# Low parts of every fourth feed-forward weight chunk by an adding DMA, and four chunks held as parts, in a two-layer encoder trunk

## The chip, the cores and the metric

The kernel runs on one core of one Trainium2 chip. The metric is the device time of one execution in microseconds (us); the time of before is the median of three runs.

## The reference

Input x is [1, 256, 2048] in float32: 256 positions, 2048 features. Layer 0 is a mixer (a Conformer convolution beside a gated spatial unit, one input and one output projection) and a SwiGLU feed-forward; layer 1 is a Fourier mixer with a linear map, and a second feed-forward; a final RMSNorm follows. Of it, what the change touches is the feed-forward, with D_FF = 5632:

```python
def swiglu(h, w_gate, w_up, w_down):
    return (jax.nn.silu(h @ w_gate) * (h @ w_up)) @ w_down

h = rms_norm(x, ffn_norm_g[layer])
x = x + swiglu(h, ffn_w_gate[layer], ffn_w_up[layer], ffn_w_down[layer])
```

All of it is to float32 accuracy.

## The kernel before, in words

Activations lie with features on the partitions and the 256 positions on the free axis, so each 128x128 weight tile is the stationary operand of TensorE as it lies in memory. A float32 product is carried by three passes: each operand is split exactly into a high and a low part of at most 12 significant bits (float32r), and TensorE accumulates wh*xh, wh*xl and wl*xh. In `product` (L252) the first two are one pass of 512 columns with wh stationary (L257), the third is one pass of 256 columns with wl stationary (L258). `products` and `extend` (L261 to L273) do the same with three passes of 256 columns. So of each weight tile TensorE needs wh first and wl right behind it.

The weights are one stream of 656 chunks (`NCHUNK`) in the order of use. A chunk is eight weight tiles side by side, 128 partitions x 1024 float32, 512 KB. `Weights.load` (L97) does three things for a chunk: SyncE issues the transfer into a `raw` tile (L104), ScalarE casts it to the high part `whi` (L105), and VectorE subtracts the high part from the raw chunk, which gives the low part `wlo` (L106). `Weights.chunk` (L133) loads chunks until three beyond the one in use are in hand (AHEAD = 3), and hands out the chunk in use. There are four `raw` buffers (RAWS) and three buffers each of `whi` and `wlo` (PARTS). With three, the parts of chunk c are written into the buffers of chunk c-3, so the cast of c waits until TensorE has done with c-3, that is, until it starts on chunk c-2. The framework puts the instructions of each engine into a fixed order when the program is built, by their dependences and buffers; on the chip each engine takes its instructions strictly in that order and waits at semaphores.

The stream is used in this order: the mixer of layer 0 (96 chunks), the first feed-forward (264 chunks), the map of the Fourier mixer (32 chunks), the second feed-forward (264 chunks). In `ffn` (L329) each of the 44 tiles j of the hidden layer takes 2 chunks for the gate and 2 for the up product (176 chunks in all), then `joined` (L286, called twice), a sigmoid (L340), two products on VectorE (L341, L342) and a split of the result into an operand `h` (L278, L280). The 16 tiles m of the down product take the other 88 chunks, each followed by `residual` (L318) and the next norm's operand (`part_of_norm`, L165 and L167, and the squares, L189 and L196).

Operands come from one pool of 2 KB tiles per partition, tag `op`, with 60 buffers (KF + KD, L82). A feed-forward fills all of them: 16 of the norm's operand and 44 of `h`. Between the two feed-forwards the Fourier mixer reads two constant matrices; `dsp` (L625) holds the parts of one of them, 8 KB per partition in the constant pool, written from a `raw` buffer by L633 and L634 and read by `positions` (L667 to L669). GpSimd does little in this kernel: constants at the start, and the power -0.5 of the norms' means (L301, 14 times).

Of the kernel before, what the change touches and what calls it, by code (L numbers as in the profile page):

```python
"""Two-layer hybrid encoder trunk (conv + spatial gating, then FNet), float32, one core.

Activations live on chip with features on the partitions and the 256 positions on the free
axis, so that every weight matrix is the stationary operand as it lies in memory and no
activation has to be transposed.  A float32 product is carried by three single passes of
TensorE: each operand is split exactly into two parts of at most 12 significant bits (float32r),
x = xh + xl and w = wh + wl, and wh*[xh | xl] (one 512 column pass) and wl*xh are accumulated in
float32.  The norms' factors per position commute with the products and are applied to their
results, so that TensorE doesn't wait for them.
"""  # L10
# [7 lines left out]
F32 = mybir.dt.float32  # L18
# [6 lines left out]
S = 256            # positions  # L25
NB = S // P        # blocks of 128 positions
D = 2048
KD = D // P        # 16 feature tiles
DFF = 5632
KF = DFF // P      # 44  # L30
CD = 1024
KC = CD // P       # 8
TAPS = 31
PAD = 15
GD = 256           # channels of an FNet group
NG = D // GD
NV = CD // 512
CH = 8             # weight tiles of 128x128 to a chunk
AHEAD = 3          # chunks that are split ahead of the one in use
RAWS, PARTS = 4, 3 # chunks in flight as they come, and as their two parts  # L40
NMISC = 3          # PSUM banks beside those of the products with the weights
PAIRS = 11         # pairs of the convolution's taps whose products are ScalarE's
OPEN = 5           # output tiles of the first projection that stay in PSUM between its parts
LAST = 2           # convolution tiles that are taken in last for them
# the pace of the work beside the products in the first mixer, in chunks (ticks)
BUDGET = 2.0       # VectorE's work beside the split of a chunk
LATE = 1           # pairs of tiles by which the squares of x come after its split
R_AT = 4           # the first norm's factors
DELAY = 3          # before TensorE reads what VectorE is to have done
GAP = 2            # between the steps of a chain over several engines  # L50
NORM_GAP = 3       # the same in the convolution's norm
NCHUNK = (4 * KD * KC + 2 * KC * KD + KD * KD + 2 * 3 * KD * KF) // CH
RMS_EPS = 1e-6
LN_EPS = 1e-5

# columns of the packed vectors that lie along the partitions
# [10 lines left out]
def trunk(ctx, tc, xT, vec, sgu_gb, sgu_bs, sgu_wT, w, dft_c, dft_s, out):  # L67
# [12 lines left out]
    def op(dt=F32R, shape=(P, 2 * S), name="op"):  # L80
        """A 2 KB tile: an operand's two parts, or what lives beside them."""
        return acts.tile(list(shape), dt, name=name, tag="op", bufs=KF + KD)  # L82

# [6 lines left out]
    # ---- weights: one stream of chunks in the order of use, split ahead of it, and the work that  # L90
    # goes on beside the products, in the order in which the engines take it up ----
    class Weights:
        def __init__(self):
            self.loaded, self.used, self.ready = 0, 0, []
            self.tick, self.tasks, self.later, self.credit = 0, [], [], 0.0

        def load(self, pieces=1):  # L97
            raw = raws.tile([P, CH * P], F32, name="raw")
            hi = wts.tile([P, CH * P], F32R, name="whi")
            lo = wts.tile([P, CH * P], F32R, name="wlo")  # L100
            n = CH * P // pieces
            for i in range(pieces):
                c = slice(i * n, (i + 1) * n)
                nc.sync.dma_start(raw[:, c], w[self.loaded][:, c])  # L104
                nc.scalar.copy(hi[:, c], raw[:, c])  # L105
                nc.vector.tensor_sub(lo[:, c], raw[:, c], hi[:, c].bitcast(F32))  # L106
            self.loaded += 1
            self.ready.append((hi, lo))

        def start(self, task, ticks=1):  # L110
            """A generator to be taken up in so many ticks; it yields the ticks until its next part
            and what the part before is to VectorE."""
            self.tasks.append((self.tick + ticks, task))

        def step(self):
            """One tick: the parts that are due, and then of the work without haste what fits."""
            self.credit = min(self.credit, 0.0) + BUDGET
            due = [x for x in self.tasks if x[0] <= self.tick]
            self.tasks = [x for x in self.tasks if x[0] > self.tick]
            for _, task in due:  # L120
                r = next(task, None)
                if r is not None:
                    self.credit -= r[1]
                    self.start(task, r[0])
            while self.later and self.credit > 0:
                cost = next(self.later[0], None)
                if cost is None:
                    self.later.pop(0)
                else:
                    self.credit -= cost  # L130
            self.tick += 1
# [38 lines left out]
    class Norm:  # L170
        """An RMSNorm over the features: its operand's parts, without the factor per position, as
        the residual's tiles come in.  The squares are summed up by VectorE in all tiles but the
        last."""
# [5 lines left out]
        def parts(self, k, x):  # L179
            """In two parts, the second for VectorE."""  # L180
# [71 lines left out]
    def product(xs):  # L252
        """sum over tiles of w.T @ x: columns 0:S and S:2S of a PSUM bank are its two parts."""
        acc = ps.tile([P, 2 * S], F32, name="acc")
        for k, x in enumerate(xs):
            wh, wl = next(stream)
            nc.tensor.matmul(acc, wh, x, start=k == 0, stop=False)  # L257
            nc.tensor.matmul(acc[:, :S], wl, x[:, :S], start=False, stop=k == len(xs) - 1)  # L258
        return acc

    def products(xs, n):  # L261
        """n sums over tiles, side by side, each in one part."""
        accs = [ps.tile([P, 2 * S], F32, name="acc")[:, :S] for _ in range(n)]
        extend(accs, xs)
        return accs
# [9 lines left out]
    def split(dst, x):  # L275
        """x in its two float32r parts."""
# [9 lines left out]
    def joined(acc, name, scale):  # L286
        """The two parts of a product added, and scaled per position."""
# [8 lines left out]
    def inv_std(means, eps):  # L296
        """(mean + eps) ** -0.5 of [128 positions, 2] means."""
# [6 lines left out]
    def add_cols(m, x, one, first, last):  # L304
        """Add to m [128 positions, 2] the sums over the partitions of x [128, 256]."""
# [4 lines left out]
    def along_free(r):  # L310
        """[128, 2] per position to [128, 256], the same in each partition."""
# [6 lines left out]
    def residual(m, acc, bias=None):  # L318
        """The product's two parts (and a bias) onto the residual's tile m."""
# [42 lines left out]
    def convolution(j, y):  # L362
        """The depthwise convolution of y.  Of 2 * PAIRS taps ScalarE forms the products."""
# [34 lines left out]
    def group_norm(j):  # L398
        """LayerNorm over the group's channels, without its gain and bias."""
# [45 lines left out]
    # spatial gating: v with the positions on the partitions  # L445
# [43 lines left out]
    # W_s (n g + b) + b_s = (W_s n) g + b rowsum(W_s) + b_s, whose gain and bias lie on partitions  # L489
# [90 lines left out]
    # the output projection: first what comes from the gating, then from the convolution  # L580
# [40 lines left out]
    # cos of channels 0..128 and sin of 1..127 hold all of a real group's channel transform  # L621
# [3 lines left out]
    dsp = const.tile([P, 2, NB, 2, S], F32R, name="dsp")  # L625
# [6 lines left out]
    for f in range(2):  # L632
        nc.scalar.copy(dsp[:, f, :, 0, :], dsr[:, f])  # L633
        nc.vector.tensor_sub(dsp[:, f, :, 1, :], dsr[:, f], dsp[:, f, :, 0, :].bitcast(F32))  # L634
# [26 lines left out]
    def positions(g, ab):  # L661
        pq = bank()
        for f in range(2):
            o = pq[:, f * S:(f + 1) * S]
            for b in range(NB):
                ah, al = ab[0][:, b, f * P:(f + 1) * P], ab[1][:, b, f * P:(f + 1) * P]
                nc.tensor.matmul(o, ah, dsp[:, f, b, 0, :], start=b == 0, stop=False)  # L667
                nc.tensor.matmul(o, ah, dsp[:, f, b, 1, :], start=False, stop=False)
                nc.tensor.matmul(o, al, dsp[:, f, b, 0, :], start=False, stop=b == NB - 1)  # L669
# [58 lines left out]
def _tiles(k, *mats):  # L728
    """Matrices [K, M] as tiles [128, 128] in the order of use: for each output tile, for each
    matrix, over K."""  # L730
# [4 lines left out]
def _side_by_side(w, n):  # L735
    """The tiles of groups of n output tiles, over K and within the group."""
# [69 lines left out]
```

## Time and profile before

| what | value |
|---|---|
| runs | 1925.70, 1927.16, 1912.75 us; median 1925.7 |
| profiled execution: span from its first to its last instruction | 1913.1 us |
| what lies around that span, against the median | 12.6 us |
| TensorE (PE) busy | 1890.0 us, 99% of the span |
| VectorE (DVE) busy | 1270.8 us, 66% |
| ScalarE (ACT) busy | 984.1 us, 51% |
| GpSimd (POOL) busy | 17.4 us, 1% |
| SyncE's DMA queue | 347.73 MB, 55.2% of 16 engines' span |

The profiled execution has no total time of its own listed; its span is given, and the difference to the median of the runs is taken for what lies around. PE is the engine's matmuls, PEld its weight loads, which overlap the matmuls. A matmul's end in the profile is modelled and rows of consecutive matmuls overlap, so TensorE's pace is read from the starts or from counts, not from the mean duration.

### The profile page before, as it was taken

The numbers are of one execution on the slowest core, as the hardware profiler recorded it, in microseconds if no ns is written. First come the engines' busy times: TensorE is split into PE (matmuls) and PEld (weight loads), VectorE is DVE, ScalarE is ACT, GpSimd is POOL, SyncE is SP. The second block draws the span as 40 slices with busy tenths as digits, with TensorE's granted clock in tenths as the row PEclk, the third lists the DMA queues.
The fourth block names the chain that finished last, engine by engine and source line by source line (L and its number), as shares of the span: only waits on it lengthen the run. The fifth ranks groups of instructions, "written<-read, shape, count | busy, mean of one in ns | idle before, by whom it ended". The sixth has DMA issues, their size and how long they took to land.

```text
span 1913.1 us, 29269 instructions
## 1 busy us (share of the span) xinstructions
PE 1890.0 (99%) x11520; PEld 1680.2 (88%) x11520; DVE 1270.8 (66%) x1860; ACT 984.1 (51%) x1504; POOL 17.4 (1%) x46
## 2 busy tenths in 40 slices
PE   8999999999999999999999999999999999999997
PEld 8989999888888888888888888888888888888887
DVE  7999856666666666655555776666666666655554
ACT  8988745444444444444444654444444444444442
POOL 0000000000000000000000000000000000000000
PEclk9999999999999999999999999999999999999999
DMA  7555554555555555555556255555555555555553
GB/s 246 168 165 164 165 180 168 193 188 189 191 193 187 189 191 192 188 188 190 194 188 196 86 187 177 188 191 193 187 189 191 191 189 188 191 193 188 188 190 129
DMA packets 98321, 351.56 MB, mean 184 GB/s; under 512 B 11268, under 2 KB 12420, under 8 KB 98184
## 3 DMA queue, kind: packets, MB, share of 16 engines
q1 hardware_dynamic: 97464, 347.73, 55.2%
q8 instruction: 90, 1.47, 0.3%
q10 hardware_dynamic: 720, 1.97, 0.3%
q14 instruction: 47, 0.39, 0.1%
HBM read 347.54 MB, written 2.10 MB: 183 GB/s over the span
## 4 chain that ended last, share of the span: by engine, by line
PE 97%; DVE 1%; ACT 1%; issue 0%; DMA 0%; POOL 0%; SPq 0%; POOLq 0%; DVEq 0%; ACTq 0%
PE acc L257 54%; PE acc L258 27%; PE acc L271 4%; PE acc L273 4%; PE acc L272 4%; PE acc L484 1%; PE acc L485 1%; PE acc L486 1%; PE m L307 0%; DMA raw<-in_w 0%; DVE wlo L106 0%; PE m L314 0%; ACT whi L105 0%; PE m L667 0%; DVE res L723 0%
## 5 line engine op out<-in xcount | busy, mean ns | idle before, releaser
L257 PE MATMUL acc<-op,whi 128*128 128x512 f32 x4436 | 1541.9, 394 | 1.0 <-ACT whi L105 1.0
L258 PE MATMUL acc<-op,wlo 128*128 128x256 f32 x4436 | 1230.5, 278 | 0.1
L106 DVE TENSOR_TENSOR wlo<-raw,whi 128x1024 fp32r<-128x1024 f32 (+1 forms) x659 | 803.9, 1220 | 565.4 <-ACT whi L105 562.7
L105 ACT CAST whi<-raw 128x1024 fp32r<-128x1024 f32 (+1 forms) x659 | 688.2, 1044 | 876.4 <-issue 506.6
L257 PEld LDWEIGHTS acc<-op,whi 128*128 128x128 f32 x4436 | 832.4, 188 | 195.4 <-ACT whi L105 1.3
L258 PEld LDWEIGHTS acc<-op,wlo 128*128 128x128 f32 x4436 | 833.7, 188 | 1.1 <-DVE wlo L106 0.7
L271 PE MATMUL acc<-op,whi 128*128 128x256 f32 x684 | 196.8, 288 | 6.2 <-ACT whi L105 5.7
L273 PE MATMUL acc<-op,wlo 128*128 128x256 f32 x684 | 194.2, 285 | 1.3 <-DVE wlo L106 1.2
L272 PE MATMUL acc<-op,whi 128*128 128x256 f32 x684 | 194.9, 285 | 0.0
L271 PEld LDWEIGHTS acc<-op,whi 128*128 128x128 f32 x684 | 132.3, 194 | 7.2 <-ACT whi L105 6.0
L273 PEld LDWEIGHTS acc<-op,wlo 128*128 128x128 f32 x684 | 131.9, 193 | 1.9 <-DVE wlo L106 1.9
L272 PEld LDWEIGHTS acc<-op,whi 128*128 128x128 f32 x684 | 132.5, 194 | 0.5 <-DVE op L167 0.2
L375 ACT ACTIVATE op<-op,vt 128x256 f32<-128x256 f32 x168 | 72.4, 499 | 0.0
L289 ACT COPY l<-acc 128x256 f32<-128x256 f32 x176 | 64.8, 368 | 0.0
L392 DVE TENSOR_TENSOR op<-op 128x512 f32<-128x512 f32 x80 | 53.8, 684 | 1.6 <-ACT op L375 1.2
L278 ACT CAST op<-a 128x256 fp32r<-128x256 f32 x112 | 43.9, 398 | 10.3 <-DVE a L543 9.4
L280 DVE TENSOR_TENSOR op<-a,op 128x256 fp32r<-128x256 f32 x112 | 46.3, 419 | 2.0 <-ACT op L278 1.8
L292 DVE TENSOR_TENSOR a<-a,nR 128x256 f32<-128x256 f32 x88 | 37.5, 426 | 6.5 <-ACT nR L210 3.5
L292 DVE TENSOR_TENSOR b<-b,nR 128x256 f32<-128x256 f32 x88 | 37.5, 426 | 3.0
L342 DVE TENSOR_TENSOR a<-a,b 128x256 f32<-128x256 f32 x88 | 37.4, 425 | 3.0
L341 DVE TENSOR_TENSOR a<-a,s 128x256 f32<-128x256 f32 x88 | 36.9, 419 | 0.0
L291 DVE TENSOR_TENSOR b<-acc,l 128x256 f32<-128x256 f32 x88 | 36.7, 417 | 0.0
(121 smaller groups left out, 708.7 us busy)
## 6 DMA issues: line engine op xcount, KB each, us to landing
raw<-in_w SPq DMA_DIRECT2D x655, 512.0 KB, 3.4
res<-in_xT SPq DMA_DIRECT2D x7, 256.0 KB, 6.6
out<-res ACTq DMA_DIRECT2D x3, 512.0 KB, 2.8
raw<-in_w SPq DMA_DIRECT2D x4, 128.0 KB, 3.2
op<-in_sgu_wT SPq DMA_DIRECT2D x2, 256.0 KB, 3.4
raw<-in_dft_s SPq DMA_DIRECT2D x1, 512.0 KB
res<-in_xT SPq DMA_DIRECT2D x2, 128.0 KB, 2.5
raw<-in_dft_c SPq DMA_DIRECT2D x1, 256.0 KB
```

The lines of the kernel that those rows point to most:

```text
L105: nc.scalar.copy(hi[:, c], raw[:, c])
L106: nc.vector.tensor_sub(lo[:, c], raw[:, c], hi[:, c].bitcast(F32))
L257: nc.tensor.matmul(acc, wh, x, start=k == 0, stop=False)
L258: nc.tensor.matmul(acc[:, :S], wl, x[:, :S], start=False, stop=k == len(xs) - 1)
L271: nc.tensor.matmul(acc, wh, x[:, :S], start=first and k == 0, stop=False)
L272: nc.tensor.matmul(acc, wh, x[:, S:], start=False, stop=False)
L273: nc.tensor.matmul(acc, wl, x[:, :S], start=False, stop=last and k == len(xs) - 1)
L280: nc.vector.tensor_sub(dst[:, n:2 * n], x, dst[:, :n].bitcast(F32))
L289: nc.scalar.copy(t, acc[:, S:])
L292: nc.vector.tensor_mul(y, y, scale)
L375: nc.scalar.activation(t[:, f * S:(f + 1) * S], src, AF.Copy, scale=wc)
L392: nc.vector.tensor_add(sums, sums, t)
```

## The change

Two more helpers in `Weights` and two constants decide which chunks are treated otherwise: of the two feed-forwards each chunk whose number is divisible by 4 (EVERY), without the first and the last 8 chunks of each (CH = 8 is taken as the margin). For such a chunk VectorE's subtraction is gone. ScalarE writes the negated high part into `wlo` behind its cast, and GpSimd issues a transfer of the same 512 KB that adds the chunk onto `wlo`: from the weights in HBM in the first feed-forward, from the `raw` tile in SBUF in the second. PARTS goes from 3 to 4 for all chunks. The 8 KB for it come from `dsp`, which becomes four tiles of the pool `op`. The sums and their results are the same. Comments are left out below.

```diff
-RAWS, PARTS = 4, 3
+RAWS, PARTS = 4, 4
+EVERY = 4
...
+NFFN = 3 * KD * KF // CH
+FFN = (NCHUNK - 2 * NFFN - KD * KD // CH, NCHUNK - NFFN)
...
+        def summed(self, i):
+            return i % EVERY == 0 and any(a + CH <= i < a + NFFN - CH for a in FFN)
...
                 nc.sync.dma_start(raw[:, c], w[self.loaded][:, c])
                 nc.scalar.copy(hi[:, c], raw[:, c])
-                nc.vector.tensor_sub(lo[:, c], raw[:, c], hi[:, c].bitcast(F32))
+                if self.summed(self.loaded):
+                    nc.scalar.activation(lo[:, c], hi[:, c].bitcast(F32), AF.Copy, scale=-1.0)
+                    src = w[self.loaded][:, c] if self.loaded < FFN[1] else raw[:, c]
+                    nc.gpsimd.dma_start(lo[:, c], src, accum_op=ALU.add)
+                else:
+                    nc.vector.tensor_sub(lo[:, c], raw[:, c], hi[:, c].bitcast(F32))
...
-    dsp = const.tile([P, 2, NB, 2, S], F32R, name="dsp")
+    dsp = [[op(shape=(P, 2, S)) for _ in range(NB)] for _ in range(2)]
...
     for f in range(2):
-        nc.scalar.copy(dsp[:, f, :, 0, :], dsr[:, f])
-        nc.vector.tensor_sub(dsp[:, f, :, 1, :], dsr[:, f], dsp[:, f, :, 0, :].bitcast(F32))
+        for b in range(NB):
+            d = dsp[f][b]
+            nc.scalar.copy(d[:, 0], dsr[:, f, b])
+            nc.vector.tensor_sub(d[:, 1], dsr[:, f, b], d[:, 0].bitcast(F32))
```

The three matmuls of `positions` read `dsp[f][b][:, 0]` and `dsp[f][b][:, 1]` in the same places.

## Rows read from the trace of the kernel before

**Rows 1.** The page: engines' busy time, slices, and the chain that ended last.
```profile
PE 1890.0 (99%) x11520; PEld 1680.2 (88%) x11520; DVE 1270.8 (66%) x1860; ACT 984.1 (51%) x1504; POOL 17.4 (1%) x46
...
PE 97%; DVE 1%; ACT 1%; issue 0%; DMA 0%; POOL 0%; SPq 0%; POOLq 0%; DVEq 0%; ACTq 0%
```
**Rows 2.** Windows: stretch, span, busy of PE, PEld, DVE, ACT, POOL (count), clock, DMA, GB/s.
```profile
500.00:700.00 200.00, 200.00 (x1156) 174.83 (x1155) 135.38 (x199) 96.87 (x145) 0.00 (x0) 1.00 0.58 190
700.00:900.00 200.00, 200.00 (x1156) 174.82 (x1155) 122.55 (x163) 91.76 (x124) 0.00 (x0) 1.00 0.57 190
...
1600.00:1800.00 200.00, 200.00 (x1156) 174.90 (x1155) 113.09 (x139) 89.64 (x112) 0.00 (x0) 1.00 0.59 190
```
**Rows 3.** Waits of TensorE: us in total, times, longest.
```profile
PE acc L271 <- ACT whi L105: 5.7, 2, 5.5
...
PE acc L273 <- DVE wlo L106: 1.2, 2, 0.9
PE acc L257 <- ACT whi L105: 1.0, 1, 1.0
```
**Rows 4.** Timeline of TensorE in the first down product: start, us, line.
```profile
857.20 0.27 PE L258 MATMUL acc<-op,wlo 128*128 128x256 f32 x1
857.31 0.40 PE L257 MATMUL acc<-op,whi 128*128 128x512 f32 x1
```
**Rows 5.** Timeline of ScalarE and VectorE there: start, us, line [idle before].
```profile
857.39 1.05 ACT L105 CAST whi<-raw 128x1024 fp32r<-128x1024 f32 x1 [1.68 <-PE acc L257]
860.17 1.05 ACT L105 CAST whi<-raw 128x1024 fp32r<-128x1024 f32 x1 [1.73 <-PE acc L257]
...
858.47 1.23 DVE L106 TENSOR_TENSOR wlo<-raw,whi 128x1024 fp32r<-128x1024 f32 x1 [1.50 <-ACT whi L105]
```
**Rows 6.** Timeline of ScalarE in the first gate and up products.
```profile
599.52 1.05 ACT L105 CAST whi<-raw 128x1024 fp32r<-128x1024 f32 x1 [1.45 <-issue]
600.48 0.41 ACT L340 ACTIVATE s<-a 128x256 f32<-128x256 f32 x1
602.29 1.05 ACT L105 CAST whi<-raw 128x1024 fp32r<-128x1024 f32 x1 [1.41 <-issue]
```
**Rows 7.** Groups by line and shape, of VectorE and ScalarE: busy us, mean ns | idle before.
```profile
L106 DVE TENSOR_TENSOR wlo<-raw,whi 128x1024 fp32r<-128x1024 f32 x655 | 802.3, 1225 | 564.8 <-ACT whi L105 562.2
...
L278 ACT CAST op<-a 128x256 fp32r<-128x256 f32 x112 | 43.9, 398 | 10.3 <-DVE a L543 9.4 <-DVE a L676 0.9
...
L165 ACT ACTIVATE op<-res,vt 128x256 fp32r<-128x256 f32 x64 | 31.5, 505 | 3.2 <-DMA res<-in_xT 2.0 <-DVE res L326 0.8 <-DVE res L583 0.3
```
**Rows 8.** The loads of weights (L104): all their landings, from issue.
```profile
DMA to landing us min/median/max: 2.9/3.4/7.0
```
**Rows 9.** GpSimd's power (L301): duration in ns, min/median/max.
```profile
L301 POOL TENSOR_TENSOR is_r<-is_v,mhalf x14: 690/1068/1641, 27.1 to 1902.5; 128x2 f32<-128x2 f32 x14
```
**Rows 10.** The Fourier mixer's start: writing of dsp (duration ns, starts), and its first reader.
```profile
L633 ACT CAST dsp<-raw x2: 607/611/615, 1046.9 to 1048.2; 128x512 fp32r<-128x512 f32 x2
...
1048.94 1.29 DVE L634 TENSOR_TENSOR dsp<-raw,dsp 128x512 fp32r<-128x512 f32 x2
1052.70 0.16 DVE L299 TENSOR_SCALAR is_v<-m 128x2 f32<-128x2 f32 x1 [2.48 <-PE m L307]
```

More of the change, by code (lines that the diff above doesn't have):

```diff
@@ L666, in positions @@
                 ah, al = ab[0][:, b, f * P:(f + 1) * P], ab[1][:, b, f * P:(f + 1) * P]
-                nc.tensor.matmul(o, ah, dsp[:, f, b, 0, :], start=b == 0, stop=False)
-                nc.tensor.matmul(o, ah, dsp[:, f, b, 1, :], start=False, stop=False)
-                nc.tensor.matmul(o, al, dsp[:, f, b, 0, :], start=False, stop=b == NB - 1)
+                nc.tensor.matmul(o, ah, dsp[f][b][:, 0], start=b == 0, stop=False)
+                nc.tensor.matmul(o, ah, dsp[f][b][:, 1], start=False, stop=False)
+                nc.tensor.matmul(o, al, dsp[f][b][:, 0], start=False, stop=b == NB - 1)
         return pq
```

## The prediction

> **What bounds the kernel now.** I read the page first: TensorE is busy for 1890.0 of 1913.1 us, and the chain that ended last is TensorE's for 97% [rows 1]. The reader is to see that no other engine has a share to give. Then the windows inside the two feed-forwards, to ask whether TensorE's pace depends on anything around it: in 200 us it starts 1156 matmuls while VectorE is busy for 135.38, for 122.55 or for 113.09 us, always with PE busy for all 200 us and the clock at 1.00 [rows 2], the upper level, 2.4 GHz. That is 0.346 us to a tile (two matmuls) and 2.77 us to a chunk, four chunks 11.09 us. VectorE's load can fall by 22 us in a window and TensorE doesn't go faster. Last the waits of TensorE: all that it ever waited for casts or low parts is 5.7 + 1.2 + 1.0 = 7.9 us [rows 3], and the lines L271 and L273 there belong to the mixers and the last tile. So in the feed-forwards weights come early enough, and work taken from VectorE is worth nothing by itself.
>
> **How early.** In the down product TensorE starts a chunk at 857.31 [rows 4], and 0.08 us later the cast begins that had waited for the buffer of the chunk just done; the next cast is one chunk, 2.78 us, behind it [rows 5]. With three buffers that cast is for the chunk that is used two chunks on, at 857.31 + 5.55 = 862.86. Its low part is ready at 858.47 + 1.23 = 859.70 [rows 5]: 3.2 us to spare.
>
> **The change part by part.**
>
> *Subtractions removed.* Summed chunks are 62 in each feed-forward (42 in gate and up, 20 in down): 124 x 1.225 = 152 us off VectorE [rows 7]. By the windows above this is worth 0.
>
> *Negations added.* 124 on ScalarE, each 128x1024. The cast of that size takes 1.05 us [rows 5]; a 128x256 activation with a scale takes 0.505 where the cast takes 0.398 [rows 7], so 1.05 to 1.16; I take 1.15, 143 us in all. ScalarE is busy for 96.87 of 200 us in a gate and up window [rows 2], 5.4 of 11.09 us, and goes to 6.5 of 11.09: hidden, as long as its order lets the casts come in time. What is queued behind a negation is at most the next cast, which waits 2.77 us for its buffer anyway, and one small instruction of 0.41 us [rows 6].
>
> *Four buffers of parts.* The cast of chunk c now goes when TensorE starts on chunk c-3, and c is used three chunks later, 8.32 us. For an ordinary chunk the spare time grows from 3.2 to 5.9 us. For a summed one: cast 0.08 to 1.13, negation to 2.28, and 8.32 - 2.28 = 6.0 us are left for the adding transfer, from the moment GpSimd may issue it until TensorE must have the low part (5.6 if one small instruction stands between). This margin is the number that the forecast hangs on. In the mixers four buffers can only loosen casts; the most there is to win is the 7.9 us of [rows 3], and the likeliest is near nothing, since the longest of them, 5.5 us, is a cast early in the kernel.
>
> *The adding transfer.* The trace shows none, so I bound it. From below: a plain load of 512 KB lands 3.4 us after its issue [rows 8]. From above: GpSimd takes 1.07 us for even a tiny instruction, 1.64 at most [rows 9]; the transfer must read twice as much as a plain load (the source and `wlo`); and it shares the 16 engines with the raw loads. These are at 0.58 in the windows [rows 2], and with four loads in 11.09 us one load is 0.58 x 11.09 / 4 = 1.6 us of all engines. So the upper bound is 1.64 + 3.4 + 1.6 for the second read + 1.6 for one raw load that is interleaved = 8.2 us. Nearest to it is the plain load behind a start on GpSimd: 1.07 + 3.4 = 4.5 us if the second read overlaps the first, 6.1 if it comes on top. I take the middle, 5.3 us, an estimate. It is under the margin by 0.7 us (0.3 behind a small instruction), so TensorE finds the low part there: cost 0. At the ends: 3.4 gives 0 too, since an earlier landing buys nothing; 8.2 gives 124 x 2.2 = 273 us.
>
> The trace has TensorE's wait on low parts at 1.2 us in all and no adding transfer to time [rows 3]. The Trainium skill, page "Collectives: The Full Stack", section "The bandwidth ceiling: the fold count and why AG ≠ RS ≠ AR", states that a reducing transfer is limited by its two source reads, which go through one ring, and so runs at half the rate of a copy. No run here shows it yet. By it the second read doesn't overlap, the transfer takes the 6.1 us of the upper of my two values or more, and the sum would stand at the edge of the margin: 0.1 us over the 6.0, or 0.5 over the 5.6 behind a small instruction, 12 to 62 us. That is a word against the change, and the first rival below is its consequence.
>
> *Room on the transfer engines.* Each summed chunk adds 1.6 to 3.2 us of all 16 engines in 11.09 us: 0.58 becomes 0.72 to 0.87. Under 1, and a raw load has time: its buffer comes free with the subtraction of four chunks before. In the second feed-forward `raw` is held until the sum has landed, some 7.6 us after its cast instead of 2.4; three other buffers go on turning, and SyncE waits longer at its head without ScalarE finding a chunk missing. I cost it at 0; uncovered it is the second rival.
>
> *dsp in the operands' pool.* It is written between 1046.9 and 1050.2, the norm's factors after it only reach VectorE at 1052.70 [rows 10], and its reader is later still. Its four tiles now wait for `h` tiles that the last down product reads first. The same 2 x 0.61 and 2 x 0.65 us of work, in halves; 0, at worst 2 us once.
>
> *Sum.* 0 + 0 + 0 (or up to -7.9) + 0 + 0: span 1913.1 us, and with the 12.6 us around it the median, 1925.7. A measurement here tells about 1% (19 us) from no change; the three runs shown lie 0.75% apart.
>
> **The rivals.**
>
> *A: the sum lands late (slower).* Place: the first low part of each summed chunk, 124 times. Nothing recovers such a wait, since the cast of the next summed chunk is itself released by TensorE. If the second read comes on top and half a raw load is interleaved, the transfer takes 1.07 + 3.4 + 1.6 + 0.8 = 6.9 us, 0.9 over the margin: 124 x 0.9 = 112 us, 2037. It decides from 6.15 us on (0.155 x 124 = 19 us). For it: DMA is already at 0.58, landings reach 7.0 us [rows 8]. Against: that maximum is one of 659, the median is 3.4.
>
> *B: held raw buffers delay the second feed-forward.* If the load four chunks on takes the very buffer that is held, a loop closes: load 3.4, cast 1.05, negation 1.15, sum 5.3, starts 0.3 = 11.2 us against 11.09, which is nothing; with a sum of 6.0 us it is 0.8 x 62 = 50 us, 1976. Against: four buffers, of which three are free in time.
>
> *C: the transfer engines become the bound.* The room is 0.42 x 11.09 = 4.7 us per summed chunk. If adding costs as much as four plain loads, 6.4 us, it is 1.7 x 124 = 211 us over, 2137. Nothing in the trace speaks for so much.
>
> *D: a small gain.* Four buffers end all 7.9 us of waits: 1918, which is within 1%.
>
> **How the numbers follow.** Forecast 0.50, with a range of its own from 1912 to 1945 (the waits of the mixers on one side, a sum that is 0.15 us late on the other). A 0.29, B 0.08, C 0.06, D 0.07, of which 0.04 for a measurement that shows it as over 1%. Faster 0.04; same 0.50 + 0.03 = 0.53; slower 0.29 + 0.08 + 0.06 = 0.43. The range goes from 1908 to 2070: above it lie C and the upper third of A, below it next to nothing, under 0.2 together.
>
> **What would show it right or wrong.** Right: windows in the feed-forwards still with 1156 matmuls in 200 us, no TensorE wait at L258, VectorE about 152 us less, ScalarE about 143 us more, DMA between 0.72 and 0.87 there. The landing of GpSimd's transfers, by the listing of DMA issues, should be under 6 us. Wrong: a wait of L258 on a DMA, 124 or 62 times (A or B), fewer matmuls in a window, casts that wait for raw loads, or a DMA share near 1 (C).

## The result and the profile after

The changed kernel takes 1973.6 us, median of four runs (1968.5 to 1974.2). Against the kernel before, of which there are now four runs with a median of 1919.9 us, it is slower by a ratio of 1.0275, 95% interval 1.0234 to 1.0317. The profiled execution took 1968.5 us for a span of 1966.7 us: only 1.8 us lie around a span, not the 12.6 us that the table ahead of the prediction takes. What those 12.6 us were comes below.

The page after, to be laid beside [rows 1]; the third and fourth lines are the transfer queues (packets, MB, share of 16 engines), the last two the landings (median us from issue).
```profile
PE 1915.3 (97%) x11520; PEld 1689.9 (86%) x11520; DVE 1126.8 (57%) x1738; ACT 1105.1 (56%) x1630; POOL 125.3 (6%) x170
...
PE 75%; DMA 10%; issue 9%; ACT 3%; DVE 2%; POOL 0%; SPq 0%; POOLq 0%; DVEq 0%; ACTq 0%
...
q1 hardware_dynamic: 97464, 347.73, 50.6%
q0 software_dynamic: 17856, 65.02, 19.1%
...
wlo<-in_w POOLq DMA_DIRECT2D x62, 512.0 KB, 5.9
wlo<-raw POOLq DMA_DIRECT2D x62, 512.0 KB, 4.8
```
The reader is to see three things. DMA and "issue" now stand in the chain that ended last, with 19% together; before, TensorE had 97% of it. TensorE lies idle for 1966.7 - 1915.3 = 51.4 us, before for 23.1 us: 28.3 us of the 53.6 us by which the span grew are idle time. And it is busy for 25.3 us longer with the same 11520 matmuls: most of that is pace, and the rest, as the late chunk below shows, is a part of the waits that the rows count as busy.

TensorE's waits after (L269 and L270 are now the lines of the high and the low passes, L257 and L258 before), for [rows 3], and windows after, for [rows 2] (stretch, span, busy of PE, PEld, DVE, ACT, POOL, clock, DMA, GB/s).
```profile
PE acc L270 <- DMA wlo<-in_w: 25.7, 26, 1.5
...
PE acc L270 <- DMA wlo<-raw: 1.7, 1, 1.7
```
```profile
600.00:800.00 200.00, 194.88 (x1103) 168.49 (x1102) 110.47 (x173) 108.31 (x156) 14.86 (x17) 1.00 0.79 226
...
1400.00:1600.00 200.00, 200.00 (x1133) 173.33 (x1133) 112.63 (x178) 112.35 (x160) 15.50 (x18) 1.00 0.78 231
```
The waits are in the first feed-forward, where the sum reads HBM; the second, where it reads the raw tile, has one in all. But the second isn't free either. There TensorE is busy for 200 of 200 us at a granted clock of 1.00 and starts 1133 matmuls, where before it started 1156 [rows 2]: a tile takes 0.353 us and not 0.346. That costs some 14 us in a feed-forward of 2112 tiles, and no wait shows it.

One late chunk of the first feed-forward, in the chain that ended last (start, us, what); ahead of it the low pass that waited, with its neighbours, from TensorE's timeline.
```profile
521.09 0.39 PE L269 MATMUL acc<-op,whi 128*128 128x512 f32 x1
522.27 0.39 PE L270 MATMUL acc<-op,wlo 128*128 128x256 f32 x1 [0.80 <-DMA wlo<-in_w]
522.50 0.39 PE L269 MATMUL acc<-op,whi 128*128 128x512 f32 x1
```
```profile
512.89 0.83 ACT whi L111
513.72 0.13 issue
513.85 0.15 ACT op L290
514.00 0.15 issue
514.16 1.06 ACT wlo L114
515.22 0.29 issue
515.51 6.72 DMA wlo<-in_w
522.23 0.04 issue
522.27 0.22 PE acc L270
```
The cast, one small instruction of ScalarE (L290), the negation until 515.22, 0.29 us until GpSimd starts, and a transfer of 6.72 us. The low pass follows its high pass by 0.23 us elsewhere, so it was wanted at 521.32 and is 0.95 us late. From the end of the negation to that point there were 6.1 us.

The row of that wait says 0.80 us, but from 521.09 to 522.50 two passes take 1.41 us that take 0.35 elsewhere: the wait cost 1.06. The end of the pass ahead is modelled, and the difference counts as busy time. By the starts of L269 in the whole trace the two feed-forwards lost some 34 us at waits and some 21 us by pace (7 in the first, 13 in the second), and the rest of the kernel gave 1 us back.

### The profile page after: what moved, and what is told of

Same layout as the page of the kernel before. It is cut to its first block, busy times and chain, and to the rows that moved or that the text cites. A ratio compares the mean times of both kernels' runs of the same rounds, so it can differ in the third digit from the quotient of the medians.

```text
span 1966.7 us, 29529 instructions
## 1 busy us (share of the span) xinstructions
PE 1915.3 (97%) x11520; PEld 1689.9 (86%) x11520; DVE 1126.8 (57%) x1738; ACT 1105.1 (56%) x1630; POOL 125.3 (6%) x170
## 3 DMA queue, kind: packets, MB, share of 16 engines
q1 hardware_dynamic: 97464, 347.73, 50.6%
## 4 chain that ended last, share of the span: by engine, by line
PE 75%; DMA 10%; issue 9%; ACT 3%; DVE 2%; POOL 0%; SPq 0%; POOLq 0%; DVEq 0%; ACTq 0%
PE acc L269 40%; PE acc L270 21%; DMA wlo<-in_w 10%; PE acc L283 4%; PE acc L285 4%; PE acc L284 4%; ACT wlo L114 1%; ACT whi L111 1%; PE acc L496 1%; PE acc L497 1%; PE acc L498 1%; DVE wlo L118 0%; DVE op L404 0%; DMA wlo<-raw 0%; PE m L326 0%
## 5 line engine op out<-in xcount | busy, mean ns | idle before, releaser
L269 PE MATMUL acc<-op,whi 128*128 128x512 f32 x4436 | 1561.4, 397 | 0.0
L270 PE MATMUL acc<-op,wlo 128*128 128x256 f32 x4436 | 1247.1, 281 | 28.4 <-DMA wlo<-in_w 25.7
L118 DVE TENSOR_TENSOR wlo<-raw,whi 128x1024 fp32r<-128x1024 f32 (+1 forms) x535 | 651.6, 1219 | 638.5 <-ACT whi L111 635.9
L269 PEld LDWEIGHTS acc<-op,whi 128*128 128x128 f32 x4436 | 832.5, 188 | 200.1 <-DVE a L693 0.4
L270 PEld LDWEIGHTS acc<-op,wlo 128*128 128x128 f32 x4436 | 837.6, 189 | 39.3 <-DMA wlo<-in_w 35.4
L285 PE MATMUL acc<-op,wlo 128*128 128x256 f32 x684 | 194.2, 285 | 1.7 <-DVE wlo L118 1.7
L114 ACT ACTIVATE wlo<-whi 128x1024 fp32r<-128x1024 f32 x124 | 131.1, 1057 | 1.0
L116 POOL DMA_DIRECT2D wlo<-in_w x62 | 54.4, 878 | 667.7 <-ACT wlo L114 667.7
L116 POOL DMA_DIRECT2D wlo<-raw x62 | 53.5, 862 | 644.4 <-ACT wlo L114 632.0
L301 ACT COPY l<-acc 128x256 f32<-128x256 f32 x176 | 64.1, 364 | 0.0
L290 ACT CAST op<-a 128x256 fp32r<-128x256 f32 x112 | 44.3, 402 | 10.5 <-DVE a L555 9.6
L313 POOL TENSOR_TENSOR is_r<-is_v,mhalf 128x2 f32<-128x2 f32 x14 | 14.3, 1019 | 518.1 <-DVE is_v L311 518.1
```

Of the source, the lines that this page charges most:

```text
L114: nc.scalar.activation(lo[:, c], hi[:, c].bitcast(F32), AF.Copy, scale=-1.0)
L116: nc.gpsimd.dma_start(lo[:, c], src, accum_op=ALU.add)
L285: nc.tensor.matmul(acc, wl, x[:, :S], start=False, stop=last and k == len(xs) - 1)
L301: nc.scalar.copy(t, acc[:, S:])
```

## The experiments

Theory: a sum from HBM lands late, and each wait may leave TensorE in a slower rhythm. Rivals: the four buffers themselves, the load of the transfers, the source. Before each timed group the kernel before ran on the same chip.

**1. Four buffers and dsp alone.**
```diff
-            return i % EVERY == 0 and any(a + CH <= i < a + NFFN - CH for a in FFN)
+            return False and any(a + CH <= i < a + NFFN - CH for a in FFN)
```


> The change's four buffers and the new place of dsp, with no adding transfer at all. Theory (late sums, and a slower rhythm of TensorE that a wait may leave behind): no TensorE wait at the low parts in the feed-forwards; each feed-forward runs either at 1156 matmuls in 200 us, as before, or at 1133, whichever rhythm it falls into after the wait on the norm's factors; time 1912 to 1942 us, a ratio of 0.995 to 1.015. Rival (four buffers or the tiles' new addresses slow TensorE): 1133 matmuls in 200 us in both feed-forwards from the start, about 27 us over before, whatever else happens.

Ratio 0.9995 (0.9956 to 1.0034). Its windows are those of before, one of the second feed-forward:
```profile
1400.00:1600.00 200.00, 200.00 (x1156) 174.90 (x1155) 135.72 (x199) 96.65 (x144) 0.00 (x0) 1.00 0.55 190
```
So buffers and addresses cost and win nothing that shows (the interval is within 0.5%). The runs beside it say more. The 19 runs of the kernel before fall on three levels: 7 between 1911.8 and 1915.6 us, 9 between 1926.9 and 1929.2, 3 between 1939.6 and 1942.5. The ten of this kernel do the same (2, 6, 2). The steps are 13 to 14 us, about what one feed-forward at 0.353 us a tile costs; no run of the kernel before on an upper level was profiled, so this is read from the times and from experiment 4. The first three runs shown of before were two of the middle level and one of the lowest, and the profiled execution, with both feed-forwards at 1156, belongs to the lowest: that, and not something around the span, was the 12.6 us.

**2 and 3. The source of the sum.** The raw tile in both feed-forwards, or HBM in both:
```diff
-                    src = w[self.loaded][:, c] if self.loaded < FFN[1] else raw[:, c]
+                    src = raw[:, c]
```
```diff
-                    src = w[self.loaded][:, c] if self.loaded < FFN[1] else raw[:, c]
+                    src = w[self.loaded][:, c]
```


> The change with the raw tile in SBUF as the source of the adding transfer in both feed-forwards. Theory (the sum from HBM lands at the edge of its margin, the one from SBUF 1.2 us inside it): the waits of L270 on the transfer in the first feed-forward, 25.7 us, go to under 4; what is left over before is TensorE's rhythm, 0 to 28 us; time 1914 to 1945 us. Rival (the transfers cost by their load on the engines or on GpSimd, wherever they read from): the first feed-forward keeps most of its loss, time over 1960 us.

> The change with HBM as the source of the adding transfer in both feed-forwards. Theory: the second feed-forward now waits as the first does, 62 more transfers with about half of them late by about 1 us each, 25 to 35 us more than the change: 1990 to 2010 us. Rival (the first feed-forward's waits come from its place or its order of instructions, not from the source): the second stays without waits, 1965 to 1978 us.

From the raw tile: 1930.9 us, ratio 1.0036 (0.9987 to 1.0086), no difference that can be told, and runs again on three levels (1919 to 1921, 1931, 1941 to 1943). From HBM: 2009.4 us, 1.0434 (1.0368 to 1.0500). The wait of TensorE on the sums, and all their landings (the issues of L116); the raw tile first, then HBM:
```profile
PE acc L270 <- DMA wlo<-raw: 1.7, 1, 1.7
```
```profile
DMA to landing us min/median/max: 4.5/4.8/6.0
```
```profile
PE acc L270 <- DMA wlo<-in_w: 64.5, 69, 1.8
```
```profile
DMA to landing us min/median/max: 5.0/6.4/7.6
```
Both as the theory has it. What 124 sums from the raw tile cost is too little to tell: at most 0.9% by the interval, and level against level some 1 to 6 us. What the change loses beyond that and beyond the rhythm comes with HBM as the source, or with what its raw buffer, free early there, lets through; experiment 8 parts the two.

**4. Late low parts without any transfer.** The kernel before; 15 chunks of the second feed-forward get their low part through four more negations on ScalarE, so the values are the same and late.
```diff
+LATE_AT = range(400, 640, 16)
...
                 nc.vector.tensor_sub(lo[:, c], raw[:, c], hi[:, c].bitcast(F32))
+                if self.loaded in LATE_AT:
+                    for _ in range(3):
+                        nc.scalar.activation(lo[:, c], lo[:, c].bitcast(F32), AF.Copy, scale=-1.0)
+                    nc.scalar.activation(lo[:, c], lo[:, c].bitcast(F32), AF.Copy, scale=-1.0)
```


> The kernel before, with no adding transfer; the low part of each sixteenth chunk of the second feed-forward (15 chunks) passes four more times through ScalarE, negated each time, so that it comes late. Theory (TensorE falls into one of two rhythms after a wait, whatever made it wait): 15 waits of 0.5 to 2.5 us at the low part; between them some stretches run at 1156 matmuls in 200 us (0.346 us a tile) and some at 1133 (0.353 us), though nothing is added by DMA. Rival (the adding transfers or GpSimd slow TensorE's reading): the pace between the waits stays at 0.346 us a tile everywhere.

One run, 1985.4 us. TensorE waited 15 times for those low parts, 14.1 us, and 12 times for casts that came late behind the negations, 20.2 us, which I hadn't expected. Windows, first the untouched first feed-forward, then two stretches between waits:
```profile
400.00:600.00 200.00, 200.00 (x1134) 173.41 (x1133) 133.43 (x196) 94.74 (x141) 0.00 (x0) 1.00 0.54 186
...
1360.00:1396.00 36.00, 36.00 (x209) 31.50 (x208) 24.54 (x36) 17.97 (x28) 0.00 (x0) 1.00 0.55 192
1598.00:1634.00 36.00, 36.00 (x206) 31.23 (x205) 23.87 (x35) 17.37 (x27) 0.00 (x0) 1.00 0.56 190
```
There are two rhythms, 1156 and 1133 to 1134 matmuls in 200 us (209 and 206 in 36), with no adding transfer in the kernel and GpSimd idle. The first feed-forward, whose instructions are those of before, has the slower one (1134 at 600 to 800 us too). So the rhythm isn't the transfers' doing.

**5. Halves.** The change, each summed chunk in two halves.
```diff
+            if self.summed(self.loaded):
+                pieces = 2
             n = CH * P // pieces
```


> The change, HBM as source in the first feed-forward, but each summed chunk in two halves (load, cast, negation and adding transfer for 4 tiles each). Theory (the sum from HBM is only late, by about 1 us at the first tile): the first half's transfer is issued about 1.1 us earlier and is half as long, the second half is needed 1.4 us later, so the waits of L270 on the transfer go from 25.7 us to under 4; time 1914 to 1945 us by TensorE's rhythm. Rival (reading these chunks twice from HBM costs by itself, through slower raw loads): over 1960 us.

1943.1 us, ratio 1.0135 (1.0102 to 1.0167). The time is in the theory's range, but the waits on HBM's sums fall from 25.7 to 10.9 us, not under 4. The page has 6.2 us to the landing of a half from HBM and 4.1 from the raw tile, but these are medians over first and second halves, which are issued 0.55 us apart. One by one in the trace, a first half lands after 5.4 us and a second after 6.8 from HBM, and after 3.3 and 4.6 from the raw tile. So the half that is needed first does come sooner, by 0.5 us from HBM and by 1.5 us from the raw tile (against 5.9 and 4.8 for a whole sum); from HBM that isn't enough for all. The second feed-forward of this profile ran at 1134, so some 14 us of what is left is rhythm.

**6. Three buffers of parts, raw tile as source.**
```diff
-RAWS, PARTS = 4, 4
+RAWS, PARTS = 4, 3
```


> The raw tile as source in both feed-forwards, but three buffers of parts instead of four. Theory (the sum lands about 7.15 us after the buffer came free, whatever the buffers): use comes 5.5 us after that instead of 8.3 to 8.5, so each of 124 sums is 1.4 to 1.7 us late: 175 to 210 us of waits, time 2090 to 2150 us. Rival (order or load, not the lead, decides): within 20 us of the four-buffer run, 1919 to 1960 us.

TensorE's wait on the sums:
```profile
PE acc L270 <- DMA wlo<-raw: 188.2, 124, 4.6
```
2153.2 us in one run. All 124 sums are late, by 1.5 us in the mean of the rows, as the lead of 5.5 us says: the fourth buffer is what pays for the transfer. (The time is 3 us above the expected range. By the starts of L269 a wait costs 1.8 us, 225 us in all, because the rows count a part of it as busy; the slower rhythm adds 12.)

**7 and 10. The passes of two tiles paired.** The kernel before, with both 512 column passes ahead of both 256 column passes.
```diff
-        for k, x in enumerate(xs):
-            wh, wl = next(stream)
-            nc.tensor.matmul(acc, wh, x, start=k == 0, stop=False)
-            nc.tensor.matmul(acc[:, :S], wl, x[:, :S], start=False, stop=k == len(xs) - 1)
+        for k in range(0, len(xs), 2):
+            two = [next(stream) + [xs[k + i]] for i in range(2)]
+            for i, (wh, wl, x) in enumerate(two):
+                nc.tensor.matmul(acc, wh, x, start=k + i == 0, stop=False)
+            for i, (wh, wl, x) in enumerate(two):
+                nc.tensor.matmul(acc[:, :S], wl, x[:, :S], start=False, stop=k + i == len(xs) - 1)
```


> The kernel before, no transfers added; in the product of two parts the passes of two weight tiles are paired: both 512 column passes, then both 256 column passes. If TensorE's two rhythms (1156 or 1133 matmuls in 200 us) come from how a weight load fits under the short pass, the paired order has another rhythm and the three levels of time (1912, 1927, 1942 us) go or move. If they come from the sum of passes and loads alone, the count stays at 1133 to 1156 in 200 us and the time at 1912 to 1942 us.

> The paired passes once more, to see them beside runs of the kernel before that have several levels. If paired passes have one rhythm only (1150 matmuls in 200 us), all runs lie within 1918 to 1924 us, while the kernel before lies at 1912 to 1916 or, in other runs, near 1927 or 1941. If they have two rhythms as well, some runs lie some 13 us or 27 us higher.

The first time every run of before was on its lowest level (1913.2 to 1915.5) and the pairs took 1919.6, ratio 1.0032 (1.0019 to 1.0045). The second time before had 16 runs up to 1916.2, 9 near 1929 and 2 above 1941; the pairs' 12 runs lay between 1918.7 and 1921.0, ratio 1.0000 (0.9972 to 1.0028). Their windows show 1150 or 1151 in nearly every stretch. So another order of loads and passes has another rhythm, though the runs don't show by what; pairing trades three levels for one between the first and the second, and beats the kernel before only where that isn't on its lowest.

**8. HBM as source, raw buffer held.** A tiny instruction of GpSimd reads the raw tile and the finished sum, so the next load can't take the buffer before the sum has landed. Otherwise as experiment 3.
```diff
                     nc.gpsimd.dma_start(lo[:, c], src, accum_op=ALU.add)
+                    seen = small.tile([P, 2], F32, name="seen")
+                    nc.gpsimd.tensor_tensor(seen, raw[:, :2], lo[:, :2].bitcast(F32), op=ALU.add)
```


> HBM as source of every sum, as in the run with HBM in both feed-forwards (64.5 us of waits, 2009 us), but the raw buffer is held until the sum has landed, by a tiny instruction of GpSimd that reads two columns of it and of the sum. Theory (the sum is late because the raw load that the freed buffer lets through 1.2 us after the release shares the transfer engines with it): without that load beside it the sum lands as early as one from SBUF, waits of L270 on the transfer under 5 us, 1914 to 1945 us. Rival (reading the source from HBM is itself slower): the waits stay near 64 us and the time over 1990 us.

The same two views of it, TensorE's wait and the landings (L116):
```profile
PE acc L272 <- DMA wlo<-in_w: 2.2, 2, 2.0
```
```profile
DMA to landing us min/median/max: 5.1/5.4/6.2
```
1936.1 us, ratio 1.0065 (1.0028 to 1.0102). The waits go from 64.5 to 2.2 us though every sum still reads HBM. Reading HBM as such is worth 0.6 us of landing (5.4 against 4.8), which the margin bears; the other 1.0 us (6.4 against 5.4) goes with the raw load that the freed buffer let through. In experiment 3 SyncE issues such a load 1.5 us ahead of the sum at 120 of 124 chunks, here at none.

**9 and 12. One more copy beside each sum, within SBUF.** Raw tile as source; SyncE copies the high part to an unused tile, issued behind the cast (9), or behind the negation by way of a tiny ScalarE copy (12).
```diff
+                    extra = acts.tile([P, CH * P], F32, name="extra")
+                    nc.scalar.copy(extra[:, :2], lo[:, :2].bitcast(F32))
                     nc.gpsimd.dma_start(lo[:, c], src, accum_op=ALU.add)
+                    nc.sync.dma_start(extra, hi.bitcast(F32))
```
(9 is without the ScalarE line.)

> The raw tile as source in both feed-forwards (1931 us, 1.7 us of waits), and beside each sum one plain copy of 512 KB from the high part in SBUF to an unused tile in SBUF, issued by SyncE behind the cast; nothing more is read from HBM. Theory (the engines are shared packet by packet, wherever the bytes come from): sums are again late in both feed-forwards, 25 to 70 us of waits of L270 on the transfer, 1955 to 2015 us. Rival (it is HBM that is shared): the waits stay under 5 us and the time at 1914 to 1945 us.

> As the run with one extra copy of 512 KB from SBUF to SBUF beside each sum from the raw tile, but the copy is issued only behind the negation (it waits for a tiny ScalarE instruction that reads the negated part, 2.5 us or later after the release instead of 1.2), so that it is on the engines while the sum is. Theory (the engines are shared, whatever the bytes come from): the sum now lands 5.7 us or more after its issue instead of 4.8 to 4.9, about 0.2 to 0.5 us late at many of the 124 chunks: 15 to 60 us of waits of L270 on the transfer, time 1945 to 2010 us. Rival (only reading from HBM slows it): landing at 4.8 to 5.0 us, waits under 6 us, time 1914 to 1947 us.

Experiment 9 came out at the rival's numbers: 4.6 us of waits and 1939.7 us; the 25 to 70 us of the theory didn't come. The two views, then a copy and its sum, with a raw load and its sum of experiment 3 below for comparison (start us, us, what):
```profile
PE acc L272 <- DMA wlo<-raw: 4.6, 3, 2.5
```
```profile
DMA to landing us min/median/max: 4.6/4.9/8.2
```
```profile
711.27 0.47 SPq L118 DMA_DIRECT2D extra<-whi  x1
712.81 0.87 POOL L116 DMA_DIRECT2D wlo<-raw  x1 [10.45 <-ACT wlo L114]
...
718.31 0.33 SPq L110 DMA_DIRECT2D raw<-in_w  x1
719.84 0.87 POOL L116 DMA_DIRECT2D wlo<-in_w  x1 [10.43 <-ACT wlo L114]
```
The copy stands where the raw load of experiment 3 stands, 1.5 us ahead of the sum, in both runs at 120 of 124 chunks, and takes about as long to land (4.1 us in the median, 4.3 for the loads of experiment 3). The transfer engines are busier with it (0.91 in the window from 600 to 800 us, 0.77 in experiment 3). Yet in the median the sum lands only 0.1 us later than without it (4.9 against 4.8), where the raw load cost 1.0 us. One by one, a copy that lands within 2.2 us of the sum's start leaves the sum at 4.8 us, and one that lands after 2.75 us makes 5.5 of it; with the raw loads of experiment 3 the two groups have 5.2 and 6.5. So the copy does slow a sum while it is under way, but by about half of what a raw load does.

In 12 the copy goes 0.3 us ahead of the sum. The same two views (the sum is at L118 there):
```profile
PE acc L273 <- DMA wlo<-raw: 39.0, 98, 3.3
```
```profile
DMA to landing us min/median/max: 5.5/6.1/7.1
```
2004.1 us, 1.0404 (1.0314 to 1.0494), waits and landings as the theory said. So a neighbour that reads nothing from HBM can make a sum late when it goes just ahead of it. That the raw load of experiment 3 does all its harm in this way isn't shown: at its distance the copy did much less. That HBM, read by the load and the sum at once, adds to it is the rival that stays; no run has a raw load 1.5 us ahead of a sum that reads SBUF.

**11. The change once more.** 


> The change itself once more beside the others, unedited. Theory: 25 to 35 us of waits in the first feed-forward and 0 to 28 us of rhythm over the fastest runs of before: 1955 to 1980 us.

1978.9 us, ratio 1.0306 (1.0261 to 1.0352), 38.9 us of waits on sums (37.2 from HBM, 1.7 from the raw tile). The time is in the expected range, the waits on HBM's sums are 2 us above theirs.

## Why the prediction was wrong

The forecast was no change, at 0.53. What happened is in the main rival A, the late sum, which it gave 0.29, in the first feed-forward alone, and beside it a slower pace of TensorE that no rival had. That the time lies inside the range is no merit: the range went from 1908 to 2070 us, rival A's waits came to a third of their price, and the pace, which no term had, added the rest.

- *The bound and its reading* held: work off VectorE is worth nothing. L106's 802.3 us [rows 7] became 650.1 for the same shape at L118, 152 us less as worked out, and TensorE is none the faster. Negations took 1.06 us where I had 1.15, 131 us in all.
- *The margin* held: 6.1 us in the chunk shown. A small instruction stands between there, so the forecast to compare is 5.6, which was 0.5 us too small. One piece was left out of it, the 0.29 us between the end of the negation and GpSimd's start.
- *The step that failed is the adding transfer at 5.3 us*, the middle between 4.5 and 6.1. It measured 4.8 from the raw tile and 5.9 from HBM (6.4 and 6.5 in the runs 3 and 11). With the 0.3 us ahead of it the first is inside the margin, the second at its edge, where 26 of 62 come late by 1.0 us in the mean (25.7 / 26). The two sources stood in the diff, and I gave them one price.
- *The second read comes on top in the engines' time, not in the landing.* The queues' shares give 0.191 x 1966.7 / 124 = 3.0 us of 16 engines for a sum and 0.506 x 1966.7 / 663 = 1.5 us for a plain load (347.73 MB are 663 times 512 KB). The Trainium skill, "Collectives: The Full Stack", section "The bandwidth ceiling: the fold count and why AG ≠ RS ≠ AR", has the reducing transfer of a collective at half the rate of a copy for its two reads; this trace agrees in the engines' time. But a sum with no load issued just ahead of it landed after 4.8 us (raw tile) and 5.4 us (HBM), both under the 6.1 that I had for a second read on top.
- *What decides is what lies beside the sum*, and this I had only as "half a raw load". Landings go from 5.4 to 6.4 us when a raw load is issued 1.5 us ahead of a sum from HBM (experiments 8 and 3), and from 4.8 to 6.1 us with a copy within SBUF 0.3 us ahead (12), but only to 4.9 with the copy 1.5 us ahead (9). The Trainium skill, "DMA: Bandwidth & Descriptors", section "Issuing engines are not separate DMA queues", says that transfers issued by GpSimd and by SyncE run on the same 16 engines and interleave; experiment 12 agrees (6.1 against 4.8), and by experiment 9 this alone needn't give the raw load's 1.0 us.
- *Rival B had the sign wrong.* I feared the held raw buffer of the second feed-forward. Holding it keeps the next raw load from being issued just ahead of the sum; with HBM as the source that alone took the waits from 64.5 to 2.2 us (experiment 8).
- *Room on the engines* was right: 0.79 and 0.78 in the windows shown, 0.72 to 0.87 forecast. Rival C didn't occur.
- *The pace taken as fixed* was the other fault. I read 1156 matmuls in 200 us from one execution and took it for a constant, and the 0.75% between the runs for noise. It is a level: the same instructions run at 1133. In the change's profile some 21 us of 53.6 are that pace, 13 of them in the second feed-forward. Rival A's price of 112 us had none of it and sized the waits, some 34 us, at three times their length: it had the lateness of a late sum about right (0.9 us) and all 124 late, where the rows have 27.

What picks the rhythm after a wait stays open. It needs no sum: the times of run 1 and of the kernel before show all levels, and the first feed-forward of experiment 4 the slower rhythm. How much of the change's mean loss is rhythm can't be separated for each run, since only profiled ones show it.

## What to carry to other kernels

A transfer whose landing must meet a margin is priced with what else is on the engines at that moment: look for the event that starts the neighbour, here a buffer that the cast set free some 1.6 us before the sum was issued, and hold that buffer if the sum is the one that matters. Price two sources as two transfers. And before a time difference of a per cent is explained, count the matmuls in equal windows of a stretch that should be steady: busy time and waits show nothing of a slower rhythm, and the rows of waits can leave out a part of a wait, so take both from the starts of the instructions.

## What the runs showed of the hardware that I hadn't expected

- With passes of 512 and 256 columns in turn, each with its weight load, TensorE holds one of two rhythms, 1156 or 1133 to 1134 matmuls in 200 us, both with PE busy throughout and a granted clock of 1.00, and keeps it, nearly always until the next wait (in the change's profile it changed near 968 us with no wait in the rows). The three levels of the kernel before, near 1914, 1928 and 1941 us, fit it, while nothing in the instructions differs. Paired passes hold 1150.
- An adding transfer of 512 KB takes GpSimd 0.86 to 0.89 us to issue and lands 4.8 us after the start of that when its source is in SBUF and no transfer was issued in the 1.6 us ahead, 5.4 us from HBM. A raw load 1.5 us ahead makes 6.4 of the 5.4, a copy within SBUF at the same distance 4.9 of the 4.8.
- Of a sum in two halves, issued 0.55 us apart, the first landed after 5.4 us and the second after 6.8 from HBM, after 3.3 and 4.6 from the raw tile.
- A row of TensorE's waits can hold less than the wait costs: 0.80 of 1.06 us in the chunk shown.
